# RMSNorm over 16,384 rows of 512: transfers cut into other pieces, and another split of the last group of rows

## The chip, the cores and the metric

One core of a Trainium2 chip. The metric is the device time of one execution in microseconds (us), lower is better. The span in a profile is some 1.8 us shorter than that time. The times here have, roughly, two levels: most executions of a kernel lie within 0.6 us of its fastest, and with most kernels some lie 1.5 to 2.8 us higher (none did in the six runs of a2 and of c1, described below); a few lie between. I call a run *undisturbed* if it is within 1.0 us of the fastest run of the same kernel in the same job. The granted clock was 1.0 in every run. The labels fast and slow, which the official ratios use, leave some of the higher runs among the fast ones; so I give both the official ratio and the mean of the undisturbed runs.

## The reference

```python
def reference(x, gamma):            # x: 16 x 1024 x 512 float32, gamma: 512
    rms = np.sqrt(np.mean(x ** 2, axis=-1, keepdims=True) + 1e-5)
    return (x / rms * gamma).astype(np.float32)
```

The input is 33.6 MB and so is the output.

## The kernel before

The rows form four tiles of 128 partitions x 32 rows x 512. There are three slots; the fourth tile takes slot 0 again once the first tile has been stored. The tiles are worked on in groups of rows: ScalarE squares, VectorE sums, then each group's rows are shared out: the last `share` rows are scaled and multiplied by gamma on GpSimd, the others are scaled row by row on ScalarE and multiplied on VectorE. All transfers are issued by SP, in the order of the program.

```python
pieces = (0, 128, 224, 320, 416, D)
load(0, 0, 0, 8)                                   # tile, slot, first row, end
for c0, c1 in zip(pieces, pieces[1:]):             # gamma, five pieces
    nc.sync.dma_start(out=gamma_row[:, c0:c1], in_=gamma.unsqueeze(0)[:, c0:c1])
load(0, 0, 8, 16)
load(0, 0, 16, 32)
load(1, 1, 0, 16)
load(1, 1, 16, 32)
# ... (cut)
groups = [(0, 0, 7, (7,), 3), (0, 7, 9, (9,), 5), (0, 16, 16, (7, 9), 7),   # tile, row, rows, pieces, share
          # ... (cut)
          (3, 16, 16, (7, 5, 4), 3)]
# square_sums (cut): the squares of a 9-row piece go to rows 23..31 of slot 2, as scratch

def transfers(t, g):                               # after each group
    if (t, g) == (0, 0):
        store(0, 0, 0, 1)
        load(2, 2, 0, 16)
        store(0, 0, 1, 2)
        load(2, 2, 16, 23)
    elif (t, g) == (0, 16):
        store(0, 0, 2, 3)
        load(2, 2, 23, 32)
        store(0, 0, 3, 16)
        store(0, 0, 16, 32)
        load(3, 0, 0, 16)
        load(3, 0, 16, 32)
    elif (t, g) == (1, 16):
        store(1, 1, 0, 32)
    elif (t, g) == (2, 16):
        store(2, 2, 0, 32)
    elif (t, g) == (3, 0):
        store(3, 0, 0, 16)
    elif (t, g) == (3, 16):
        store(3, 0, 16, 32)

# main loop (cut), for each group
scale_by_pool(rstd, t, g, n, share)
# ... squares of the next group (cut)
scale(rstd, t, g, 0, half)
# ... (cut)
scale(rstd, t, g, half, mine)
times_gamma(t, g, 0, mine)
transfers(t, g)
```

## Time and profile before

| | before |
|---|---|
| time, median of 4 runs | 161.40 us (161.28 to 161.51) |
| span of the profiled run | 159.6 us |
| DMA engines occupied | 98.2% |
| busiest compute engine | VectorE, 70% |

The prediction below shows the page's lines. Two more from the same kernel: the number of packets (the DMA view), and the first instruction that waits for data (order of instructions: start, length, engine, line, operation, and in brackets the idle time before it and what ended it).

```profile
DMA packets 2747, 67.12 MB, mean 421 GB/s; under 512 B 313, under 2 KB 314, under 8 KB 698
```

```profile
7.88 3.16 ACT L96 ACTIVATE sq_psum<-slot 128x3584 f32<-128x3584 f32 x1 [5.24 <-DMA slot<-in_x_dram]
```

A *packet* is one partition's share of one transfer; the page's count also holds the completion records, one for each engine and transfer (309 of the 2747). The trace records start, length and bytes of each, without the number of the engine. From these records I split the time of the 16 engines in two: the packets' *own time* (8 ns a packet, 0.03677 ns a byte, 9 ns for a completion record, which is what undisturbed packets of all sizes took), and the *waits*, which is what packets took above that. Both are given per engine, as the sum over all packets divided by 16.

### The profile page before, as it was taken

How to read it: one execution, taken by the hardware profiler on the slowest of the kernel's cores; microseconds unless marked ns; L12 is line 12 of the kernel's file. 1: busy time of each engine (PE TensorE's matmuls, PEld its weight loads, DVE VectorE, ACT ScalarE, POOL GpSimd, SP SyncE). 2: the span in 40 equal slices, each digit the busy share in tenths (PEclk: the TensorE clock that was granted, in tenths of full speed). 3: DMA queues.
4: the chain of work that ended last, by engine and by line, in shares of the span. 5: the costliest groups of instructions: out<-in, count | busy, mean ns of one | idle time of the engine just before them, and what ended most of it. 6: DMA issues, size and time to landing. Idle time of an engine off the chain costs nothing.

```text
span 159.6 us, 275 instructions
## 1 busy us (share of the span) xinstructions
PE 2.0 (1%) x2; PEld 0.5 (0%) x2; DVE 112.0 (70%) x39; ACT 107.8 (68%) x108; POOL 106.4 (67%) x24
## 2 busy tenths in 40 slices
PE   0050000000000000000000000000000000000000
PEld 0010000000000000000000000000000000000000
DVE  0028097998898999999999999999999009700000
ACT  3072957967999998999899899989960990000000
POOL 1000942994999599999999999999999990000000
DMA  5999999999999999999999999996996997999995
GB/s 199 428 427 501 419 394 435 485 394 394 460 394 394 429 454 407 427 452 452 468 394 394 509 411 394 526 526 263 526 509 279 526 476 312 394 468 452 394 435 222
DMA packets 2747, 67.12 MB, mean 421 GB/s; under 512 B 313, under 2 KB 314, under 8 KB 698
## 3 DMA queue, kind: packets, MB, share of 16 engines
q1 hardware_dynamic: 2746, 67.11, 98.2%
q14 instruction: 1, 0.01, 0.0%
HBM read 33.56 MB, written 33.55 MB: 421 GB/s over the span
## 4 chain that ended last, share of the span: by engine, by line
DVE 59%; ACT 22%; DMA 4%; ACTq 0%; issue 0%
DVE ss L97 36%; DVE slot L122 23%; ACT slot L118 8%; ACT slot L96 7%; ACT sq_psum L96 6%; DMA slot<-in_x_dram 4%; DVE ss L103 1%; ACT ss L102 1%; ACTq L208 0%; ACT gamma_b L165 0%
## 5 line engine op out<-in xcount | busy, mean ns | idle before, releaser
L109 POOL TENSOR_TENSOR slot<-slot,ss 128x3584 f32<-128x3584 f32 (+2 forms) x9 | 46.9, 5214 | 23.7 <-DVE ss L103 23.7
L110 POOL TENSOR_TENSOR slot<-slot,gamma_b 128x3584 f32<-128x3584 f32 (+2 forms) x9 | 59.3, 6585 | 0.7
L97 DVE TENSOR_REDUCE ss<-sq_psum 128x7 f32<-128x3584 f32 (+1 forms) x13 | 42.2, 3246 | 13.2 <-ACT sq_psum L96 13.2
L118 ACT ACTIVATE slot<-slot,ss 128x512 f32<-128x512 f32 x75 | 47.2, 706 | 4.7 <-DVE ss L103 4.7
L122 DVE TENSOR_TENSOR slot<-slot,gamma_psum 128x4608 f32<-128x4608 f32 (+2 forms) x9 | 41.3, 4590 | 8.7 <-ACT slot L118 8.7
L96 ACT ACTIVATE sq_psum<-slot 128x3584 f32<-128x3584 f32 (+1 forms) x13 | 34.6, 2658 | 6.0 <-DMA slot<-in_x_dram 5.2
L97 DVE TENSOR_REDUCE ss<-slot 128x9 f32<-128x4608 f32 x3 | 14.9, 4953 | 4.4 <-ACT slot L96 4.2
L97 DVE TENSOR_REDUCE ss<-sq_sbuf 128x5 f32<-128x2560 f32 x5 | 14.0, 2802 | 0.0
L96 ACT ACTIVATE slot<-slot 128x4608 f32<-128x4608 f32 x3 | 12.1, 4032 | 0.0
L96 ACT ACTIVATE sq_sbuf<-slot 128x2560 f32<-128x2560 f32 x5 | 11.6, 2320 | 0.0
L102 ACT ACTIVATE ss<-ss,eps_t 128x16 f32<-128x16 f32 (+2 forms) x9 | 2.7, 304 | 11.9 <-DVE ss L97 11.9
L103 DVE RECIPROCAL ss<-ss 128x16 f32<-128x16 f32 (+2 forms) x9 | 2.1, 235 | 0.4 <-ACT ss L102 0.4
L66 PE MATMUL gamma_psum<-gamma_row,ones_col 1*128 1x512 f32 x2 | 2.0, 1121 | 8.7 <-DMA gamma_row<-in_gamma_dram 8.7
L72 ACT ACT_TABLE_LOAD x1 | 1.3, 1283 | 1.1 <-PEq L197 1.1
L165 ACT COPY gamma_b<-gamma_psum 128x512 f32<-128x512 f32 x1 | 0.6, 564 | 0.0
L66 PEld LDWEIGHTS gamma_psum<-gamma_row,ones_col 1*128 1x128 f32 x2 | 0.5, 304 | 8.7 <-issue 8.7
L64 POOL MEMSET ones_col<- 1x128 f32 x1 | 0.2, 194 | 0.3 <-POOLq L197 0.3
L197 POOL MEMSET const-float32-0.0<- 128x1 f32 x1 | 0.1, 98 | 0.2 <-issue 0.2
L72 ACT ACTIVATE table<-eps_t 128x1 f32<-128x1 f32 x1 | 0.2, 203 | 0.0
L197 POOL MEMSET const-bfloat16-1.0<- 128x1 bf16 x1 | 0.1, 101 | 0.0
L197 POOL MEMSET const-uint8-127<- 128x1 uint8 x1 | 0.1, 101 | 0.0
L197 POOL MEMSET const-float32-1.0<- 128x1 f32 x1 | 0.1, 98 | 0.0
(1 smaller groups left out, 0.1 us busy)
## 6 DMA issues: line engine op xcount, KB each, us to landing
slot<-in_x_dram SPq DMA_DIRECT2D x6, 4096.0 KB, 21.7
out_dram<-slot SPq DMA_DIRECT2D x3, 4096.0 KB, 21.9
slot<-in_x_dram SPq DMA_DIRECT2D x2, 2048.0 KB, 8.5
out_dram<-slot SPq DMA_DIRECT2D x1, 3328.0 KB, 21.7
slot<-in_x_dram SPq DMA_DIRECT2D x1, 2304.0 KB, 14.2
slot<-in_x_dram SPq DMA_DIRECT2D x1, 1792.0 KB
out_dram<-slot SPq DMA_DIRECT2D x3, 256.0 KB, 29.4
gamma_row<-in_gamma_dram SPq DMA_DIRECT2D x4, 0.4 KB
```

The lines of the kernel that those rows point to most:

```text
L66: nc.tensor.matmul(gamma_psum[:, 0], ones_col, gamma_row, start=True, stop=True)
L72: nc.scalar.activation(out=table, in_=eps_t, func=AF.Sqrt)
L96: nc.scalar.activation(out=sq[:, :m], in_=rows, func=AF.Square)
L97: nc.vector.tensor_reduce(out=ss[:, r : r + m, 0], in_=sq[:, :m], axis=mybir.AxisListType.X, op=OP.add)
L102: nc.scalar.activation(out=ss[:, :n, 0], in_=ss[:, :n, 0], func=AF.Sqrt, bias=eps_t, scale=1.0 / D)
L103: nc.vector.reciprocal(out=ss[:, :n, 0], in_=ss[:, :n, 0])
L109: nc.gpsimd.tensor_tensor(out=part, in0=part, in1=by_row, op=OP.mult)
L110: last = nc.gpsimd.tensor_tensor(out=part, in0=part, in1=gamma_b.to_broadcast([P, share, D]), op=OP.mult)
L118: nc.scalar.activation(out=x[:, g + r, :], in_=x[:, g + r, :], func=AF.Copy, scale=rstd[:, r])
L122: scaled = nc.vector.tensor_tensor(out=part, in0=part, in1=gamma_psum.to_broadcast([P, r1 - r0, D]), op=OP.mult)
L165: nc.scalar.copy(out=gamma_b[:, 0], in_=gamma_psum[:, 0])
L197: nc = _bacc.Bacc("TRN2", target_bir_lowering=False, num_devices=1)
```

## The change

Its intent, by its parts: fewer and larger transfers on a queue that is always full, and a last group that ends sooner, so that the last tile may be stored in one piece.

```diff
-    for c0, c1 in zip(pieces, pieces[1:]):
-        nc.sync.dma_start(out=gamma_row[:, c0:c1], in_=gamma.unsqueeze(0)[:, c0:c1])
+    nc.sync.dma_start(out=gamma_row, in_=gamma.unsqueeze(0))
@@
-        (3, 16, 16, (7, 5, 4), 3),
+        (3, 16, 16, (7, 5, 4), 5),
@@ def transfers
             store(0, 0, 0, 1)
-            load(2, 2, 0, 16)
-            store(0, 0, 1, 2)
-            load(2, 2, 16, 23)
+            load(2, 2, 0, 20)
         elif (t, g) == (0, 16):
-            store(0, 0, 2, 3)
-            load(2, 2, 23, 32)
-            store(0, 0, 3, 16)
+            load(2, 2, 20, 32)
+            store(0, 0, 1, 16)
@@
-        elif (t, g) == (3, 0):
-            store(3, 0, 0, 16)
         elif (t, g) == (3, 16):
-            store(3, 0, 16, 32)
+            store(3, 0, 0, 32)
@@ main loop
         scale(rstd, t, g, 0, half)
+        if not ahead:
+            times_gamma(t, g, 0, half)
@@
-        times_gamma(t, g, 0, mine)
+        times_gamma(t, g, 0 if ahead else half, mine)
```

More of the change, by code (lines that the diff above doesn't have):

```diff
@@ L52 @@
     gamma_row = const.tile([1, D], fp32)
-    pieces = (0, 128, 224, 320, 416, D)
     load(0, 0, 0, 8)
-    for c0, c1 in zip(pieces, pieces[1:]):
-        nc.sync.dma_start(out=gamma_row[:, c0:c1], in_=gamma.unsqueeze(0)[:, c0:c1])
+    nc.sync.dma_start(out=gamma_row, in_=gamma.unsqueeze(0))
     load(0, 0, 8, 16)
```

## The prediction

> **What bounds the kernel now.** I read the page's header and its DMA rows first, then the busy shares by stretch, then the chain of waits, then the order of instructions in the last 30 us, and last the transfer queue's own issues. The header and the DMA rows say what is scarce:
>
> ```profile
> span 159.6 us, 275 instructions
> PE 2.0 (1%) x2; PEld 0.5 (0%) x2; DVE 112.0 (70%) x39; ACT 107.8 (68%) x108; POOL 106.4 (67%) x24
> ...
> q1 hardware_dynamic: 2746, 67.11, 98.2%
> HBM read 33.56 MB, written 33.55 MB: 421 GB/s over the span
> ```
>
> No compute engine is above 70%, while the 16 DMA engines are occupied for 98.2% of the span. The table of stretches (length, busy time of PE, PEld, DVE, ACT, POOL, granted clock, DMA share, GB/s) shows where the other 1.8% is:
>
> ```profile
> 0.00:2.00 2.00, 0.00 (x0) 0.00 (x0) 0.00 (x0) 0.86 (x1) 0.43 (x6) 1.00 0.36 86
> 2.00:40.00 38.00, 2.04 (x2) 0.49 (x2) 22.56 (x9) 23.65 (x19) 16.78 (x5) 1.00 1.00 423
> 40.00:157.90 117.90, 0.00 (x0) 0.00 (x0) 89.48 (x30) 83.34 (x90) 89.19 (x14) 1.00 1.00 431
> 157.90:159.60 1.70, 0.00 (x0) 0.00 (x0) 0.00 (x0) 0.00 (x0) 0.00 (x0) 1.00 0.00 0
> ```
>
> The DMA share is 0.36 of the first 2 us, 1.00 from there to 157.9, and 0 in the last 1.7 us. So the engines idle only before the first byte (2 - 0.72, at about 1.28 us) and after the last one; in the packet records of the trace, too, each engine's packets follow one another without a gap from 1.28 to 157.9 us. The chain that ended last is misleading here: it is a chain of compute that ends at 138.7 us, twenty microseconds before the span does.
>
> ```profile
> 123.51 1.33 ACT slot L118 x2
> 124.84 0.61 ACTq L208
> 125.46 6.13 ACT slot L118 x10
> 131.59 0.02 issue
> 131.61 7.09 DVE slot L122
> ```
>
> What this chain controls is only when the last store may be issued. It is issued at 138.76; its data moves much later, because earlier stores stand ahead of it. Half a tile is 4.19 MB, 9.7 us at 431 GB/s, so its first byte moves near 157.9 - 9.7 = 148.2: 9.4 us of slack. The kernel is bound by the bytes and packets of the 16 engines, as long as something stands in their queues.
>
> **What the Trainium skill says.** "Perfetto Trace Analysis", section What "DMA-bound" means, tells apart a bound on the DMA engines and one on the sequencer that issues. Here it is the engines: an issue occupies SP for 0.33 to 0.44 us, and there are 24 of them. "DMA: Bandwidth & Descriptors", section Specifications, gives a fabric ceiling of 435 GB/s; the 431 measured agrees, and leaves no faster rate for a change of order to reach. The same page, section Why small descriptors are slow, states a fixed overhead per packet. The trace agrees: its packet records (one partition's share of one transfer each) have 84 ns for 2,048 bytes, 611 for 16,384, 1,213 for 32,768 and 2,418 for 65,536. The last two give (2418 - 1213) / 32768 = 0.03677 ns a byte, and 1213 - 1205 = 8 ns a packet whatever its size. "GPSIMD Engine Reference", section Performance versus the Vector engine, has an elementwise tensor_tensor 1.96 times as long as on VectorE; the trace has 5.6 us against about 2.8 for 2,560 elements, which agrees.
>
> **The change, part by part.** The bytes stay at 67.1 MB. Each of the 16 engines serves 8 of the 128 partitions, so each transfer has 8 packets on each engine, and each transfer's completion record adds 9 ns there.
>
> - First half-tile stored as 1 + 15 rows in place of 1 + 1 + 1 + 13. Per partition before: 3 x 84 + 987 = 1,239 ns (987 is the record for 26,624 bytes). After: 84 + (8 + 30,720 x 0.03677 = 1,138) = 1,222. Saved: 17 x 8 = 0.14 us on each engine.
> - Third tile loaded as 20 + 12 rows in place of 16 + 7 + 9. Before 1,213 + 535 + 686 = 2,434; after 1,514 + 912 = 2,426 (by the line above). Saved: 8 x 8 = 0.06 us.
> - Fourth tile stored whole: 2,418 in place of 2 x 1,213. Saved: 8 x 8 = 0.06 us.
> - Four fewer transfers of this kind: 4 x 9 ns = 0.04 us.
> - Gamma in one piece: the five packets are all on one engine (four of 22 ns, one of 27, five completions of 9: 160 ns); one of about 84 + 9 remains. It saves 0.07 us on one engine of 16, which need not be the last. SP issues five gamma transfers in 1.68 us; one takes a fifth of it, but the first load keeps the engines busy for 8 x 0.61 = 4.9 us meanwhile, so this is hidden.
>
> Sum: 0.30 us on the saturated path.
>
> The last group moves compute that isn't on that path. Rows: ScalarE and VectorE have 11 in place of 13, GpSimd 5 in place of 3, and VectorE multiplies 6 rows and then 5. The costs of GpSimd are in the groups by shape:
>
> ```profile
> L110 POOL TENSOR_TENSOR slot<-slot,gamma_b 128x2560 f32<-128x2560 f32 x1 | 5.6, 5604 | 0.1
> ...
> L109 POOL TENSOR_TENSOR slot<-slot,ss 128x2560 f32<-128x2560 f32 x1 | 4.5, 4456 | 5.2 <-DVE ss L103 5.2
> ```
>
> ```profile
> 117.36 7.78 POOL L110 TENSOR_TENSOR slot<-slot,gamma_b 128x3584 f32<-128x3584 f32 x1
> ...
> 125.08 2.77 POOL L109 TENSOR_TENSOR slot<-slot,ss 128x1536 f32<-128x1536 f32 x1
> 127.92 3.44 POOL L110 TENSOR_TENSOR slot<-slot,gamma_b 128x1536 f32<-128x1536 f32 x1
> 131.61 7.09 DVE L122 TENSOR_TENSOR slot<-slot,gamma_psum 128x6656 f32<-128x6656 f32 x1 [8.14 <-ACT slot L118]
> ```
>
> GpSimd starts the last group at 125.08, as it has only then finished the one before, and ends at 125.08 + 4.46 + 0.05 + 5.60 = 135.2. ScalarE needs 8.07 / 13 = 0.62 us a row: 6 rows at 127.2, 11 at 130.4. VectorE's multiply takes 2,277, 4,944 and 7,087 ns for 2,048, 4,608 and 6,656 elements, about 0.14 us and 1.04 ns an element: 3.35 for six rows, 2.81 for five, so it ends near 130.6 + 2.8 = 133.4. The group then ends with GpSimd at 135.2 where VectorE ended at 138.7: 3.5 us sooner, off the path by itself.
>
> It is needed, though, because the whole-tile store must now wait for the last group. The store ahead of it, of the third tile, has its last packet end at 138.55 in the trace of before, so at about 138.3 with what is saved earlier. A store takes about 0.35 us to issue and, as the first load shows (issue begun at 0.74, first byte at 1.28), 0.54 us to its first byte: 135.2 + 0.6 = 135.8. That leaves about 2.5 us. With the old split it would have been 138.76 + 0.54 = 139.3, a gap of 1.0 us. The share of five rows is what makes the whole store harmless.
>
> **The rivals.** First, the final store comes late and the engines run dry at 138. For it: the slack shrinks from 9.4 to 2.5 us, and whatever delays the compute chain delays GpSimd with it. Against it: 39 to 123 us is VectorE without a pause, on loads that landed long before, so nothing in the change reaches it. A slip of 1 us costs nothing, one of 4 us about 1.5: 162.6.
>
> Second, the second load of the third tile comes late. Its rows 23 to 31 are a scratch place, free only at 49.4:
>
> ```profile
> SPq L45 <- DVE ss L97: 20.1, 1, 20.1
> ```
>
> Before, the single rows and the 16 + 7 rows kept the engines fed to about 57.3 us. After: single-row packets begin at 40.95 in the records, plus 0.67 for the one row, plus 8 x 1.514 = 12.1 for 20 rows, gives 53.7. The issue at 49.4 has its first byte near 50.0, so 3.7 us are left. If compute slipped 5 us, this would cost 1 to 2 us. I find no reason for such a slip.
>
> Third, the start. Before, the two loads of the second tile waited for earlier transfers before SP issued them (a reused semaphore, 4.1 us in the queue's waits); with four fewer transfers ahead they are issued at once, by about 3.5 us. Were the deeper queue to slow the first load, which ScalarE awaits until 7.88, all compute would slip by as much: under 1 us, inside both slacks, so no time. A gain there is likewise hidden. And if the fixed cost per packet were paid differently in large ones, the saving would be 0 to 0.3 us.
>
> **Range and chances.** 161.39 - 0.30 = 161.1 us. Three runs of before span 0.23 us, and in the packet records some loads are lengthened by waits [...], about 1.0 us on each engine over the span, half of it at the start; that may fall differently. With a small chance of a gap of 1 us at the last store, the range is 160.7 to 161.6. A 2% change is 3.2 us. Faster by that would need more than the 2.9 us in which the engines idle before the first and after the last byte: 1%. Slower by that needs the last store over 5.5 us late, or two gaps: 2%. Within 2%: 97%.
>
> **What would show it.** Right: the DMA share stays 1.00 from 2 us to the end with no dip near 50 or 138; some 500 fewer packets; span near 159.3; GpSimd's last multiply ends near 135.2 and the last store is issued within 0.2 us of it; the end follows that issue by about 24 us, not by 21.6 (0.54 to the first byte, 8.39 MB at 431 GB/s or 19.4, and 1.7 of tail: that would mean an empty queue). Wrong: a stretch of low share before the last store or near 50 us, the first load landing later with the whole compute chain moved, or an unchanged time despite full engines, which would mean that packets cost nothing by number.

## The result, and the profile after

| | before | after |
|---|---|---|
| median of 4 runs | 161.40 us (161.28 to 161.51) | 161.47 us (161.34 to 161.54) |
| ratio | | 1.0003, 95% interval 0.9986 to 1.0021 |

A ratio is the mean time of one kernel's fast runs over that of the other's of the same rounds, so it isn't quite the ratio of the medians. The time lies inside the predicted range, but the 0.30 us that was to come off did not come off.

The page of the changed kernel, its header and DMA rows:

```profile
span 159.7 us, 260 instructions
PE 2.0 (1%) x2; PEld 0.5 (0%) x2; DVE 111.0 (70%) x40; ACT 106.6 (67%) x106; POOL 110.3 (69%) x24
...
DMA packets 2164, 67.12 MB, mean 420 GB/s; under 512 B 242, under 2 KB 242, under 8 KB 371
...
q1 hardware_dynamic: 2162, 67.11, 98.1%
```

There are 583 fewer packets in the page's count (2747 - 2164, of which 68 are completion records of 4 bytes), and yet the engines are occupied for as long as before: 98.1% of a span of 159.7 us, against 98.2% of 159.6. The order of instructions in the changed kernel shows the first awaited load and the last group, in two pieces, and answers on the SP queue alone show the 12-row load and the last store being issued (the last block is the last store of the kernel before):

```profile
8.15 3.16 ACT L94 ACTIVATE sq_psum<-slot 128x3584 f32<-128x3584 f32 x1 [5.51 <-DMA slot<-in_x_dram]
```

```profile
125.37 4.45 POOL L107 TENSOR_TENSOR slot<-slot,ss 128x2560 f32<-128x2560 f32 x1
127.61 6.09 DVE L120 TENSOR_TENSOR slot<-slot,gamma_psum 128x3072 f32<-128x3072 f32 x2 [3.85 <-ACT slot L116]
129.90 5.60 POOL L108 TENSOR_TENSOR slot<-slot,gamma_b 128x2560 f32<-128x2560 f32 x1
```

```profile
49.68 0.33 SPq L45 DMA_DIRECT2D slot<-in_x_dram  x1
```

```profile
135.53 0.33 SPq L49 DMA_DIRECT2D out_dram<-slot  x1
```

```profile
138.76 0.33 SPq L49 DMA_DIRECT2D out_dram<-slot  x1
```

The last group is as predicted: GpSimd ends at 129.90 + 5.60 = 135.50 (135.2 predicted), VectorE at 133.70 (133.4), and the store is issued at 135.53. All of it is 0.3 us later than predicted because the first load landed 0.27 us later. The span ends 24.2 us after the last issue, as it should with a full queue (about 24 predicted; 21.6 for an empty one). So the compute side held, and what is missing must be inside the transfers. The packet records say where:

```text
us per engine   own time   waits   of these: start   first store   third tile   rest   end of 15th / last engine
before            155.64    1.07              0.52          0.36         0.16   0.04            156.50 / 156.63
after             155.34    1.31              0.62          0.47         0.12   0.11            156.55 / 156.79
```

Times of the ends are counted from the start of the first packet. "start" is the first 6 us, "first store" the stretch from 34 to 42.5 us, where the loads of the second tile end and the first store begins, "third tile" from 42.5 to 64, where its loads alternate with stores of the first tile. The packets' own time fell by 0.30 us, to the hundredth as predicted. The waits rose by 0.24 us, and the last engine ends 0.16 us later than before. All waits of "first store" are in packets of the load ahead of it.

One correction to how I read the table of stretches: it counts a packet wholly in the stretch in which it begins. In the changed kernel, in stretches of 1 us around the beginning of the last store:

```profile
136.00:137.00 1.00, 0.00 (x0) 0.00 (x0) 0.00 (x0) 0.00 (x0) 0.00 (x0) 1.00 2.42 1049
137.00:138.00 1.00, 0.00 (x0) 0.00 (x0) 0.00 (x0) 0.00 (x0) 0.00 (x0) 1.00 0.00 0
138.00:139.00 1.00, 0.00 (x0) 0.00 (x0) 0.00 (x0) 0.00 (x0) 0.00 (x0) 1.00 2.28 983
```

1049 GB/s for 1 us is 16 packets of 65,536 bytes, 983 is 15, and nothing begins in between, as each lasts 2.42 us. A share of 0.36 in the first 2 us therefore doesn't mean engines occupied from 1.28 us on. 86 GB/s in those 2 us are 172 KB, which is ten packets of 16,384 bytes and one of 8,192 on another queue; by the records the tenth first packet begins 0.2 us after the first. So the first byte moves at about 1.75 us in before and 1.8 in the changed kernel, 1.0 us after the issue began, not 0.54, and the last packet ends later too (156.79 + 1.8 = 158.6). The times that the prediction took from packet records were counted from 1.28, so they are 0.47 us early: in before, the third tile's store ends at 139.0, not 138.55, and the tail after the last byte is 1.2 us, not 1.7. The slack of the last store changes little: the engines' third-tile store ends at 137.1 us after the first packet in the mean, so at 138.9, and 135.53 + 1.0 = 136.5 leaves 2.4 us.

### The profile page after: what moved, and what is told of

Its sections match the earlier page's. It is cut to its first block, busy times and chain, and to the rows that moved or that the text cites. A ratio compares the mean times of both kernels' runs of the same rounds, so it can differ in the third digit from the quotient of the medians.

```text
span 159.7 us, 260 instructions
## 1 busy us (share of the span) xinstructions
PE 2.0 (1%) x2; PEld 0.5 (0%) x2; DVE 111.0 (70%) x40; ACT 106.6 (67%) x106; POOL 110.3 (69%) x24
## 2 busy tenths in 40 slices
DMA packets 2164, 67.12 MB, mean 420 GB/s; under 512 B 242, under 2 KB 242, under 8 KB 371
## 3 DMA queue, kind: packets, MB, share of 16 engines
q1 hardware_dynamic: 2162, 67.11, 98.1%
## 4 chain that ended last, share of the span: by engine, by line
POOL 46%; ACT 18%; DVE 12%; DMA 5%; POOLq 4%; issue 0%
POOL slot L108 24%; POOL slot L107 22%; DVE ss L95 9%; ACT slot L94 7%; ACT sq_psum L94 6%; DMA slot<-in_x_dram 5%; POOLq L203 4%; ACT slot L116 3%; DVE slot L120 3%; ACT ss L100 1%; ACT gamma_b L158 0%; DVE ss L101 0%; POOLq L107 0%
## 5 line engine op out<-in xcount | busy, mean ns | idle before, releaser
L107 POOL TENSOR_TENSOR slot<-slot,ss 128x3584 f32<-128x3584 f32 (+2 forms) x9 | 48.6, 5404 | 24.0 <-DVE ss L101 24.0
L108 POOL TENSOR_TENSOR slot<-slot,gamma_b 128x3584 f32<-128x3584 f32 (+2 forms) x9 | 61.4, 6825 | 0.7
L116 ACT ACTIVATE slot<-slot,ss 128x512 f32<-128x512 f32 x73 | 46.0, 707 | 4.7 <-DVE ss L101 4.7
L120 DVE TENSOR_TENSOR slot<-slot,gamma_psum 128x4608 f32<-128x4608 f32 (+3 forms) x10 | 40.3, 4038 | 4.4 <-ACT slot L116 4.4
```

Source lines behind the costliest of these rows:

```text
L107: nc.gpsimd.tensor_tensor(out=part, in0=part, in1=by_row, op=OP.mult)
L108: last = nc.gpsimd.tensor_tensor(out=part, in0=part, in1=gamma_b.to_broadcast([P, share, D]), op=OP.mult)
L116: nc.scalar.activation(out=x[:, g + r, :], in_=x[:, g + r, :], func=AF.Copy, scale=rstd[:, r])
L120: scaled = nc.vector.tensor_tensor(out=part, in0=part, in1=gamma_psum.to_broadcast([P, r1 - r0, D]), op=OP.mult)
```

## The experiments

I began with four theories for the missing 0.3 us. *Chance*: the waits differ from one execution to the next. *Start*: gamma in one piece lets SP issue all first loads at once, and that slows the start. *Tail*: with 64 KB packets the engines end less evenly. *Switch*: where a store follows a load, packets at the load's end wait, and fewer, larger pieces make this worse. Each run after the first result was timed in five rounds against the kernel before on the same chip, in three jobs (a, b and c). The table has all of them; the differences are means of undisturbed runs minus those of the kernel before in the same job.

| run | ratio (95%) | mean of undisturbed, us (runs) | before, same job | difference |
|---|---|---|---|---|
| first result | 1.0003 (0.9986, 1.0021) | 161.45 (4 of 4) | 161.40 (4 of 4) | +0.05 |
| a1_after_again | 1.0002 (0.9949, 1.0056) | 161.48 (4 of 6) | 161.44 (8 of 11) | +0.04 |
| a2_gamma_alone | 0.9996 (0.9954, 1.0038) | 161.65 (6 of 6) | 161.44 | +0.21 |
| a3_first_third_alone | 1.0026 (0.9968, 1.0084) | 161.79 (5 of 6) | 161.44 | +0.35 |
| a4_last_alone | 0.9983 (0.9936, 1.003) | 161.44 (5 of 6) | 161.44 | 0.00 |
| b1_whole_store_old_split | 1.0035 (0.9962, 1.0108) | 162.41 (4 of 6) | 161.60 (5 of 11) | +0.81 |
| b2_stores_in_pieces | 1.0053 (0.9987, 1.0119) | 162.83 (3 of 6) | 161.60 | +1.23 |
| b3_no_early_store | 1.0005 (0.9934, 1.0076) | 162.25 (5 of 6) | 161.60 | +0.65 |
| b4_five_gamma | 1.0 (0.9913, 1.0088) | 161.88 (4 of 6) | 161.60 | +0.28 |
| c1_loads_20_12_only | 1.0003 (0.9966, 1.004) | 161.85 (6 of 6) | 161.56 (9 of 11) | +0.29 |
| c2_one_early_store_only | 1.0043 (0.9984, 1.0103) | 161.83 (4 of 6) | 161.56 | +0.27 |
| c3_after_third | 1.0012 (0.9953, 1.0072) | 161.55 (4 of 6) | 161.56 | -0.01 |
| c4_more_early_stores | 1.0015 (0.9961, 1.0069) | 161.67 (4 of 6) | 161.56 | +0.11 |

The official intervals of the experiments are wide, 0.4 to 0.9 per cent either way, because they hold disturbed runs; by them every run is "the same" at 2%, but for b3, which is "unclear". Undisturbed runs of one kernel in one job still spread by 0.1 to 0.6 us (b2: 0.85), so a difference of 0.1 us means nothing, and the ones of 0.2 to 0.35 us are worth something only where several runs agree. The cut at 1.0 us isn't beyond doubt: b2's six times run from 162.39 to 163.66 without a gap, and their mean, 163.17, is 1.57 us above before; and when the third job was planned a stricter cut was used, which left out a4's run at 161.79 (161.35 in place of 161.44).

The packet records of one profile of each, in us per engine. The profiled runs of a1, a3, b1 and c3 were disturbed ones (163.45 to 163.83 us), that of b2 took 163.24 us:

```text
                           own time   waits   start   first store   third tile   rest   15th / last engine
a1_after_again               155.34    1.50    0.59          0.18         0.65   0.08      156.73 / 159.06
a2_gamma_alone               155.63    1.42    0.66          0.40         0.06   0.31      156.83 / 156.85
a3_first_third_alone         155.42    1.48    0.64          0.34         0.42   0.09      156.64 / 158.97
a4_last_alone                155.57    1.19    0.54          0.37         0.16   0.11      156.60 / 157.05
b1_whole_store_old_split     155.34    1.55    0.44          0.29         0.68   0.14      158.66 / 159.14
b2_stores_in_pieces          156.36    1.48    0.52          0.35         0.39   0.22      157.69 / 158.41
b3_no_early_store            155.27    1.93    0.52          0.00         1.23   0.18      157.54 / 157.56
b4_five_gamma                155.35    1.34    0.52          0.69         0.02   0.11      156.64 / 156.72
c1_loads_20_12_only          155.57    1.39    0.51          0.27         0.53   0.07      156.94 / 157.00
c2_one_early_store_only      155.49    1.43    0.51          0.38         0.37   0.17      156.86 / 156.95
c3_after_third               155.34    1.43    0.55          0.34         0.47   0.06      156.64 / 158.78
c4_more_early_stores         155.71    1.21    0.59          0.26         0.13   0.23      156.75 / 156.85
```

### a1_after_again and c3_after_third: the changed kernel again

No edit.

> The changed kernel, unaltered, in five rounds and with a second profile. The first profiles showed that the packets' own time (8 ns each plus 0.03677 ns a byte, 9 ns a completion) fell by 0.296 us on each DMA engine, as predicted, and that waits inside packets rose by 0.24 us, with the last engine 0.2 us later against the mean. Theory 'chance' (these waits and the uneven ends are different in every execution): a ratio of about 0.998, 0.3 us faster, and in the new profile 155.34 us of packets' own time with a different sum of waits. Theories 'start', 'tail' and 'switch' (a part of the change brings the waits): a ratio of 1.000 or above again, and the waits of about 1.3 us in the same places.

> The changed kernel unaltered, a third time, to have it on the same chip and in the same rounds as the other three. Expected from the nine undisturbed runs so far: 0.05 us above before, ratio 1.000; the packets' own time again 155.34 us, and waits of 1.2 to 1.5 us on a mean engine where before has 1.07.

Over three jobs the changed kernel is 0.03 us above before ((0.05 + 0.04 - 0.01) / 3), not 0.30 below: *chance* in single runs isn't the answer, something takes the gain back regularly. The own time is 155.34 us each time, the waits 1.31, 1.50 and 1.43, against 1.07 in the one profile of before. The second and third profile are of disturbed runs; without the two long waits of one engine that the next paragraphs describe, they have 1.36 and 1.31. The expected places held less well: the waits moved between "first store" and "third tile" from profile to profile.

The profiled run of a1 happened to be a disturbed one (163.73 us), and shows what the second level of times is. Stretches of 1 us at its end, then the same of the first profile of the changed kernel:

```profile
155.50:156.50 1.00, 0.00 (x0) 0.00 (x0) 0.00 (x0) 0.00 (x0) 0.00 (x0) 1.00 2.42 1049
156.50:157.50 1.00, 0.00 (x0) 0.00 (x0) 0.00 (x0) 0.00 (x0) 0.00 (x0) 1.00 0.00 0
157.50:158.50 1.00, 0.00 (x0) 0.00 (x0) 0.00 (x0) 0.00 (x0) 0.00 (x0) 1.00 0.16 66
```

```profile
155.50:156.50 1.00, 0.00 (x0) 0.00 (x0) 0.00 (x0) 0.00 (x0) 0.00 (x0) 1.00 2.12 918
156.50:157.50 1.00, 0.00 (x0) 0.00 (x0) 0.00 (x0) 0.00 (x0) 0.00 (x0) 1.00 0.00 0
157.50:158.50 1.00, 0.00 (x0) 0.00 (x0) 0.00 (x0) 0.00 (x0) 0.00 (x0) 1.00 0.01 0
```

66 GB/s for 1 us is a single packet of 65,536 bytes. In the disturbed run, one packet begins in the last stretch, when no other does: one engine of 16 is alone for 2.33 us (159.06 - 156.73). The 15 others end 0.18 us later than in the first profile. Two packets of this profile stand out, at 58.9 and 97.9 us after the first one, with waits of 1.49 and 0.79 us: together 2.28. Both are at the end of a load with a store behind it. The records carry no engine number, but if each packet is followed to the one that begins within 4 ns of its end (or of the completion record behind it), the first of the two leads to the second, and at no step does another packet begin within 0.1 us: they are on one engine. The other disturbed profiles have such a pair at about 59 and 98 us too: a3 1.05 and 0.87 us, b1 1.02 and 0.59, c3 1.28 and 0.60 (one engine in a3 and c3; in b1 the steps can't be told apart); the undisturbed ones have no such pair. In these four ScalarE's first load also comes latest, at 8.44 to 8.54 us, against 7.84 to 8.26 in the nine profiles under 163 us. In these runs the span is therefore set by the slowest of 16 engines, not by the mean that the DMA share shows.

### a2_gamma_alone and b4_five_gamma: the start

a2 is the kernel before with

```diff
-    for c0, c1 in zip(pieces, pieces[1:]):
-        nc.sync.dma_start(out=gamma_row[:, c0:c1], in_=gamma.unsqueeze(0)[:, c0:c1])
+    nc.sync.dma_start(out=gamma_row, in_=gamma.unsqueeze(0))
```

and b4 is the changed kernel with the reverse.

> Of the change, only gamma in one piece (so the four loads behind it are issued 1.4 us sooner and without a wait). Theory 'start' (the deeper queue slows the first load; its landing took 7.39 us against 7.12): first landing at about 7.4, 0.1 to 0.3 us slower, ratio 1.001 to 1.002. Theory 'chance': within 0.1 us of before, 0 to 0.07 us faster, first landing anywhere between 7.1 and 7.4.

> The changed kernel with gamma in five pieces again, so everything of the change but this. Theory 'start' (gamma in one piece let the loads be issued at once, and costs 0.1 to 0.2 us, as the run of this part alone suggests: median 161.58 against 161.48): 0.1 to 0.2 us faster than the changed kernel, first load landing near 7.1. Theory 'chance': no difference beyond 0.1 us.

a2 was 0.21 us slower, as *start* has it, with 0.66 us of waits at the start against 0.52. But b4, which takes the suspect away from the changed kernel, was no faster: +0.28 to before, where the changed kernel has +0.03 in three other jobs. The start did return to 0.52 us of waits, and the first load was awaited until 7.84 us instead of 8.15; the time did not follow, as 0.69 us were waited at the first store. Nor does the first load follow gamma: with one piece it was awaited until 7.88 us in b3 and 7.97 in a2, with five pieces until 8.26 in a4. Either *start* is wrong, or it is too small to see. I dropped it as the cause; that gamma alone cost 0.2 us in six runs stays unexplained, and so does that the changed kernel with one piece (+0.03) is no slower than b4 with five (+0.28).

### a3_first_third_alone, c1_loads_20_12_only, c2_one_early_store_only: larger pieces in the first and third tile

c1 and c2 are the two halves of a3, each in the kernel before:

```diff
 # c1: loads of 20 and 12 rows, three single-row stores kept
-            load(2, 2, 0, 16)
+            load(2, 2, 0, 20)
             store(0, 0, 1, 2)
-            load(2, 2, 16, 23)
@@
             store(0, 0, 2, 3)
-            load(2, 2, 23, 32)
+            load(2, 2, 20, 32)
             store(0, 0, 3, 16)
 # c2: one single-row store, loads of 16, 7 and 9 rows kept
             load(2, 2, 0, 16)
-            store(0, 0, 1, 2)
             load(2, 2, 16, 23)
@@
-            store(0, 0, 2, 3)
             load(2, 2, 23, 32)
-            store(0, 0, 3, 16)
+            store(0, 0, 1, 16)
```

> Of the change, only one single-row store with the 15 rows behind it, and the third tile loaded in 20 and 12 rows; gamma and the last group as before. By number of packets: 0.20 us and 3 x 9 ns of completions less on each engine, so 0.23 us faster, ratio 0.9986. Theory 'switch' (the waits of the last load ahead of a store grow when fewer stores stand between the loads): packets' own time down by 0.23 us but no gain, ratio 1.000, with more than 0.4 us of waits near 37 us and more than 0.1 near 59 us after the first packet.

> The kernel before with only the third tile's loads changed, to 20 and 12 rows; three single-row stores remain, two of them now behind one another between the two loads. Packets: 0.07 us less on each engine. Theory 'switch' in the form 'what counts is how often a few stores interrupt the loads before the large stores come': one interruption fewer, waits between 57 and 62 us rise from about 0.06 to 0.1 to 0.4 us on a mean engine, time 0 to 0.3 us above before. Theory 'chance': waits as in before, 0.07 us faster.

> The kernel before with only two of the single-row stores taken away (1 + 15 rows); the third tile is still loaded in 16, 7 and 9 rows. Packets: 0.15 us less on each engine. Theory 'switch': the loads of 32 rows now come without a store between, so waits between 57 and 62 us of 0.1 to 0.6 us on a mean engine and a time 0 to 0.4 us above before, like the run with both parts (161.79 in the mean of its five undisturbed runs, against 161.45). Theory 'loads' (the shape of the loads brings the waits): waits as in before, 0.15 us faster.

These three are the clearest of the small ones. Their own time fell by 0.22, 0.07 and 0.15 us, as counted, and their time rose by 0.35, 0.29 and 0.27. The waits around the third tile's loads were 0.42, 0.53 and 0.37 us where before has 0.16. In c1 they lie near 51 us after the first packet, at the end of the 20-row load, just ahead of the store that follows it; in c2 and a3 they lie near 58, ahead of the large store. In before, short loads and single-row stores alternate there. The sum doesn't close to the hundredth (c1: own time -0.07 and waits +0.32 make +0.25 for a mean engine; its last engine ends 0.37 us later, 157.00 against 156.63), as the end is the slowest engine's. But three kernels, each with fewer alternations, each wait longer in this stretch in their one profile, and each are slower.

The waits are weaker evidence than the times. The changed kernel and b4 have the same transfers in this stretch as a3, and their profiles, of undisturbed runs, waited 0.12 and 0.02 us there, no longer than before; the larger values with these transfers are of disturbed runs (a1 0.65, a3 0.42, b1 0.68, c3 0.47) or of b2's at 163.24 us (0.39). So where a3's undisturbed runs lose 0.35 us isn't shown. c1 and c2, profiled undisturbed, are the two that show longer waits and a longer time together.

### a4_last_alone: the last group and the whole fourth tile

The kernel before with the last three parts of the diff above (five rows on GpSimd, two multiplies, one store for the fourth tile).

> Of the change, only the last group (five rows on GpSimd, two multiplies on VectorE) and the fourth tile stored whole. By number of packets: 0.07 us faster, ratio 0.9995; the last store issued near 135.3, 3 us ahead of its turn, so no gap. Theory 'tail' (with 64 KB packets the engines end less evenly): 0.1 to 0.2 us slower, ratio 1.001, and the last engine's end more than 0.2 us after the mean of the engines where before has about 0.3 us between mean and last.

No difference in the mean; four of the five undisturbed runs are at 161.24 to 161.43 and one at 161.79. *Tail* expected 0.1 to 0.2 us more; that isn't seen in the times. The profile's last engine ends 0.63 us after the mean of the engines (157.05 - 156.42), more than in before, 0.29 (156.63 - 156.34), but this was the run at 161.79. So this part is harmless, and a gain of 0.07 us is too small to be shown.

### b1_whole_store_old_split: is the queue really about to run dry?

The changed kernel with the last group as before:

```diff
-        (3, 16, 16, (7, 5, 4), 5),
+        (3, 16, 16, (7, 5, 4), 3),
-        if not ahead:
-            times_gamma(t, g, 0, half)
-        times_gamma(t, g, 0 if ahead else half, mine)
+        times_gamma(t, g, 0, mine)
```

> The changed kernel, but the last group as before (three rows on GpSimd, one multiply of 13 rows on VectorE), so that the whole-tile store must wait for the late multiply. The multiply ended at 138.7 us before; the changed kernel's first load landed 0.3 later, so 139.0, issue by 139.1, first byte 139.6. The queue of the changed kernel is empty 8 packets of 2.42 us before its last packet's end, at 138.5 on most engines: a gap of about 1.0 us. By the prediction's reasoning: span about 160.7, 162.4 us, 1.0 us above before, ratio 1.006, and a dip of the DMA share near 139 us. If the queue were not what bounds (a rival that the end is set by waits elsewhere): no more than 0.3 us above.

It took 0.81 us more than before where 1.0 was expected. Its profile is again of a disturbed run (163.83 us), in which the last multiply is about 1 us later than the expected 139.0 as well; the order of instructions and the stretches:

```profile
132.87 7.09 DVE L120 TENSOR_TENSOR slot<-slot,gamma_psum 128x6656 f32<-128x6656 f32 x1 [8.13 <-ACT slot L116]
140.03 0.33 SPq L49 DMA_DIRECT2D out_dram<-slot  x1
```

```profile
136.00:137.00 1.00, 0.00 (x0) 0.00 (x0) 1.00 (x1) 0.00 (x0) 0.00 (x0) 1.00 2.42 1049
137.00:138.00 1.00, 0.00 (x0) 0.00 (x0) 1.00 (x1) 0.00 (x0) 0.00 (x0) 1.00 0.00 0
138.00:139.00 1.00, 0.00 (x0) 0.00 (x0) 1.00 (x1) 0.00 (x0) 0.00 (x0) 1.00 0.00 0
139.00:140.00 1.00, 0.00 (x0) 0.00 (x0) 0.96 (x1) 0.00 (x0) 0.00 (x0) 1.00 0.16 66
140.00:141.00 1.00, 0.00 (x0) 0.00 (x0) 0.00 (x0) 0.00 (x0) 0.00 (x0) 1.00 2.15 918
```

The 16 packets that begin before 137 last 2.42 us; the last store is issued at 140.03, and 14 of its first packets begin after 140. In the changed kernel 15 began before 139 (shown above). By the records, 15 engines end the store before it at 137.1 to 137.5 us after the first packet and begin the last one at 139.1 to 139.3: they do nothing for 1.6 to 2.1 us. (The first of these packets begins at 140.87 us of the span, 0.84 us after the issue began.) The one packet in between is the late engine's, which has no gap: the disturbed runs of b1 (163.79 and 163.83) are no slower than those of before in the same job (163.45 to 164.27), since there that engine sets the end. Both rules, the queue must hold something and the slowest engine counts, are in this one run.

### b2_stores_in_pieces: does a packet cost time at all?

```diff
-            store(1, 1, 0, 32)
+            for r in range(0, 32, 4):
+                store(1, 1, r, r + 4)
```

in the changed kernel, and the same for the third tile.

> The changed kernel with the stores of the second and the third tile each cut into 8 pieces of 4 rows: 14 more transfers, 14 x 8 more packets on each engine, no other order of loads and stores. Theory 'packets' (8 ns a packet and 9 ns a completion lie on the path): 14 x (8 x 8 + 9) = 1.0 us above the changed kernel, 162.5 us, ratio to before 1.0065; packets' own time 156.36 us. If packets cost nothing by number, since another bound hides them: within 0.2 us of the changed kernel.

```profile
span 161.5 us, 279 instructions
...
q1 hardware_dynamic: 4178, 67.11, 97.8%
```

The own time is 156.36 us, as computed, and the mean of the engines' ends went to 157.29 from 156.39 of the changed kernel, 0.90 us. The time rose by 1.23 us over before in the undisturbed runs, of which there are only three (162.39, 162.85, 163.24), against 1.0 expected above the changed kernel. So packets do cost about what was counted, and no other bound hides it. That 0.3 us of them bought nothing in the changed kernel isn't because they were free.

### b3_no_early_store: what do the waits hang on?

```diff
-            store(0, 0, 0, 1)
             load(2, 2, 0, 20)
@@
-            store(0, 0, 1, 16)
+            store(0, 0, 0, 16)
```

in the changed kernel.

> The changed kernel without the early single-row store; the first half-tile is stored as 16 rows. Loads of 84 rows then follow one another, and the first store stands behind the 12-row load. Packets: 0.08 us less. Theory 'switch' (the last load packets ahead of a store wait, most ahead of the first store): the waits of 0.35 to 0.46 us a mean engine near 37 us vanish there; if the wait belongs to each switch, 0.4 us faster than the changed kernel (161.1); if it belongs to the first store alone it moves to about 57 us and the time stays. Theory 'chance': the waits near 37 us stay, as they belong to the loads.

The waits near 37 us vanish altogether (0.47 to 0.00) and come back larger at the next change from loads to stores: 1.23 us where the changed kernel had 0.12 to 0.65. The table of stretches shows the new place, 58 to 62 us, as engines that are as occupied as ever (1.02) and move less (319 GB/s). First this kernel, then the changed one:

```profile
38.00:42.00 4.00, 0.00 (x0) 0.00 (x0) 2.94 (x3) 4.00 (x2) 2.52 (x1) 1.00 0.99 426
...
58.00:62.00 4.00, 0.00 (x0) 0.00 (x0) 4.00 (x3) 3.64 (x5) 3.92 (x2) 1.00 1.02 319
```

```profile
38.00:42.00 4.00, 0.00 (x0) 0.00 (x0) 2.94 (x3) 4.00 (x2) 2.25 (x1) 1.00 0.80 291
...
58.00:62.00 4.00, 0.00 (x0) 0.00 (x0) 4.00 (x3) 3.64 (x5) 3.92 (x2) 1.00 1.09 456
```

Packets are counted where they begin, so a single row is rough, and the share of 0.80 is an effect of that. If each packet's bytes are spread over the time that it took, the records have 433 GB/s from 38 to 42 us in this kernel against 382 in the changed one, and 302 from 58 to 62 us against 420, with the engines occupied throughout. So the low rate has moved. The waits therefore belong to the change from loads to stores, not to a time or to those loads. That they are larger here may be due to the longer row of loads (84 rows) without a store; no run varies that alone. The expectation was 0.4 us faster, or no change; it was 0.65 us slower than before, with one transfer fewer. The single-row store that looks like waste pays for itself.

### c4_more_early_stores: a version to beat both

The kernel before with the changed last group, and the third tile's loads in 8, 8, 7 and 9 rows with a single-row store ahead of each.

```diff
             store(0, 0, 0, 1)
-            load(2, 2, 0, 16)
+            load(2, 2, 0, 8)
             store(0, 0, 1, 2)
+            load(2, 2, 8, 16)
+            store(0, 0, 2, 3)
             load(2, 2, 16, 23)
         elif (t, g) == (0, 16):
-            store(0, 0, 2, 3)
+            store(0, 0, 3, 4)
             load(2, 2, 23, 32)
-            store(0, 0, 3, 16)
+            store(0, 0, 4, 16)
```

> A candidate for better than both: the kernel before with the changed last group and whole fourth store (which alone had 161.35 in the mean of its undisturbed runs), and four single-row stores, with the third tile's loads in 8, 8, 7 and 9 rows between them. Packets: 0.07 us more than before. Theory 'switch' (frequent short interruptions take the waits away): waits between 36 and 62 us below the 0.5 us of before, 0 to 0.2 us faster than before. Theory 'packets alone': 0.07 us slower.

It does not: +0.11 us, no different from before within the spread. The waits from 34 to 64 us did fall, to 0.39 us (0.26 + 0.13) from 0.52 (0.36 + 0.16), but waits elsewhere rose and its own time is 0.07 us more. None of the versions is shown to be faster than the kernel before.

## Why the prediction was right or wrong

The bound was read right: the queues, not the compute chain that ends last. b1 shows the one way in which compute matters, and the last group's times were within 0.3 us of the predicted ones. The time was inside the range; but the range reached 0.2 us above before, so it held "no change" too, and says nothing for the 0.30 us.

The sum of the parts, 0.30 us, was right as a count (155.64 to 155.34 us per engine, and b2 for the price of a packet), and wrong as a change of the time, which was +0.03 us over three jobs. The step that failed is "Sum: 0.30 us on the saturated path", with what it silently took for granted: that the waits of about 1.0 us stay as they are. The prediction named them in its range as something that "may fall differently", as noise; b3 showed that they move with the order of loads and stores. They were 1.31 to 1.50 us in the changed kernel, so most of the 0.30 us went into them. One of the prediction's own signs of being wrong, "an unchanged time despite full engines, which would mean that packets cost nothing by number", came true, but what it was to mean did not hold: by b2 packets do cost. The mis-sized term is the first two parts, transfers merged in the first and third tile: counted at -0.20 us and completions, measured alone at +0.35 (c1 +0.29 and c2 +0.27 for its halves), and with the last group at +0.28 (b4). These sizes can't simply be added: with gamma in one piece as well the whole is +0.03. The whole fourth tile, counted at -0.07, measured 0.00.

"The share of five rows is what makes the whole store harmless" was half tested: b1 took away the five rows and the split multiply together. With 13 rows in two multiplies of 7 and 6, VectorE would, as an estimate, end at 131.6 + 3.3 = 134.9 us instead of 138.7 (ScalarE's last row, and the prediction's figure for six rows); that may suffice alone and was not run.

The first rival (a late last store) and the second (a late second load of the third tile: issued at 49.68, with nothing dry after it) did not come about. The third, the start, came in its harmless form: the first load was awaited 0.27 us longer, and the chain behind it was 0.3 us later inside its slack. That the deeper queue did this isn't shown (b3, with the same queue at the start, had 7.88 us, as before). The first byte at 1.28 us was a misreading of the table of stretches, and the packet records do not begin there, as the prediction says, but near 1.75.

What stays open: what made the waits of the whole change larger (there is only one profile of before to compare with); why packets at the end of a load wait when a store follows, and most at the first; why gamma in one piece alone costs 0.2 us while the whole change doesn't show the sum of its parts (+0.35 + 0.21 + 0.00, against +0.03); and why in some executions one engine falls 2.3 us behind.

## What to carry to other kernels

With full DMA engines, counting packets gave the engines' own time here to 0.01 us, but not the price of an order: look also at the places where loads give way to stores, where in c1, c2 and b3 more was waited than merging saved. The end belongs to the slowest of the engines, so a mean share of 98% can hide a microsecond or two on one, as in a1. Before a small transfer is removed as waste, run the kernel without it.

## What the Trainium skill lacked or had wrong

- "DMA: Bandwidth & Descriptors", section Why small descriptors are slow: a fixed cost per packet. The records here fit one of 8 ns from 2 KB to 64 KB, plus 9 ns for a completion record; whether it is the cost that the page means isn't shown. The page has nothing on waits at the end of a load with a store behind it: 0.18 to 0.69 us on a mean engine at the first store in the thirteen profiles with an early store, and 1.23 us at the later change where that store was taken away.
- "Perfetto Trace Analysis", section DMA Optimizations, recommends larger transfers for a kernel bound by DMA. Here, with the engines full and every packet 2 KB or more, one store of 15 rows in place of 1 + 1 + 13, and loads of 20 + 12 rows in place of 16 + 7 + 9, were 0.27 to 0.35 us slower in three runs, alone or together, and 0.03 us slower with the rest of the change. The other way round the advice held: stores cut into 4-row pieces (b2) cost 1.23 us.
- "DMA: Bandwidth & Descriptors", section Latency and other measured facts, has two of the 16 engines as usually slower; its guess at the reason is for transfers that GpSimd issues, and here SP issues all. Here one engine ended 2.1 to 2.3 us after the 15 others in three of the profiles (159.06 against 156.73, 158.97 against 156.64, 158.78 against 156.64), and times 1.8 us or more above the fastest came in 11 of 33 runs of the kernel before and 3 of 12 of the changed kernel in the experiments' jobs (a fourth, 162.78, lies between). The records carry no engine number, so whether it is one of those two is not shown.
